# An encoder trunk on one core: the cross-attention's output product by seven block products, and the order of all engines written out

## The chip, the core and the metric

One Trainium2 chip, and of it one core. The core has five engines with an instruction queue each: TensorE (PE; its weight loads are shown as PEld), VectorE (DVE), ScalarE (ACT), GpSimd (POOL) and SyncE (SP), which here does nothing but issue transfers. The metric is the device time of one execution in microseconds (us).

## The reference, cut to what matters

Two layers over x (512 rows of 1024), each with a mixer, a cross-attention into 256 memory rows and an MLP, all in float32:

```python
for l in range(DEPTH):
    h = rms_norm(x, g_mix[l]); z = h @ w_in[l]
    ...                                   # differential attention and a two-way linear recurrence
    x = x + jnp.concatenate([o, r], axis=-1) @ w_out[l]

    hq = rms_norm(x, g_xq[l]); m = rms_norm(mem, g_mem[l])
    qx = (hq @ xa_wq[l]).reshape(B, S, X_HEADS, X_HEAD_DIM)   # 4 heads of 256
    ...
    p = jax.nn.softmax(s, axis=-1).astype(vx.dtype)
    ox = jnp.einsum('bhsm,bmhd->bshd', p, vx).reshape(B, S, D_MODEL)
    x = x + ox @ xa_wo[l]                 # the product that the change is about

    hm = rms_norm(x, g_mlp[l])
    x = x + jnp.square(jax.nn.relu(hm @ mlp_w1[l])) @ mlp_w2[l]
return rms_norm(x, g_final)
```

## The kernel before

**Layout and tiles.** x is kept transposed: eight chunks `c_x0` to `c_x7` of 128 features by 512 rows. A weight tile is 128x1024, one column block of 128 outputs for all eight chunks of the contraction. Each float32 operand is split into a high part and a low part in a format that TensorE multiplies at speed, and a product is three matmuls (high·high, high·low, low·high). A weight arrives by a transfer in a `wraw` buffer (3 of them); ACT writes its high part to `whi` and DVE the rest to `wlo` (3 of each). `b` is a pool of 62 tiles of 128x512, `pt` one of 4, `mm` and `at` are the 3 + 5 banks of PSUM, into which TensorE writes.

**The cross-attention's output product** (called the XO stage below). `residual_fm` forms chunk m of `ox @ xa_wo`: 8 chunks of the contraction by 3 matmuls of 512 columns into one bank, then one DVE addition into `c_x`. The eight operands `ox` come from `XHead.pv`, two a head: PSUM is split at once into a high and a low tile. After each chunk `prep_x` splits the new x for the MLP (one ACT, one DVE instruction) and adds its square for the norm (one of each).

**Seven block products** (`seven`, line 1093 on) are already there for the MLP's second product. A pair of chunks of the contraction and both halves of the 512 rows make a 2x2 block matrix, and so does a pair of weight tiles; seven products of blocks do what eight did. `left_pair` makes the sums and differences of the activations (`a`, `kh/kl`, `s`, `u`), `right_pair` those of two weight tiles (`whi`, `wlo`, and `pt` for the intermediate sums). A product is 4 pairs by 3 matmuls of 256 columns. The seven run in three banks X, Y and Z; product 6 goes on in bank X on top of product 1, so it follows the DVE addition that reads product 1 out.

**Order.** Every operation is recorded by `Plan.record`, in the order of the program. `Plan.schedule` then places them with its own table of costs, by a key for each (time of recording less a lead; `ahead(...)` sets leads for loads, splits and attention, and `LEADS` holds one more for each operation). `Plan.emit` writes out the order found; each engine takes its own instructions in that order, and each waits for what it reads and for its buffers. All of them carry line 490, so the rows below are told apart by tile names.

Of the kernel before, what the change touches and what calls it, by code (L numbers as in the profile page):

```python
# [18 lines left out]
P = 128  # L19
S = 512  # L20
# [29 lines left out]
ATT_AHEAD = 3  # L50
SPLIT_AHEAD = 18.0
LOAD_AHEAD = 105.0
CAST_AHEAD = 28.0
NEG_AHEAD = 20.0
# [3 lines left out]
LEAD_STEPS = '#$%&()*+,-./0123456789:;<=>?@ABCDEFGHIJKLMNOPQRSTUVWXYZ[]^_`abcdefghijklmnopqrstu'  # L58
LEADS = (
    'uL63BCuGGgGGGG@@<<HGuue>d>auFOMu9Q-ZAAGA-2D-H)?NNOC*@%AD?EA#6&/,0,?CBBB,=5>BBDFA?1J1C-G;JF$80?FUFKP;'  # L60
    'eOD?AK9NLPBWOOZ``Y[S^YcRURQTTRQNPLNNNTJJPIJJLISQR[XMMXXOGHOJFMMABIQPVUkUU[[[WTPSSLLJLuuLRSCNRJJJKJEG'
    'GVSXQNMECF>lK`LLJIJIKKNK```KCDDIDcCjL[YSeY_Ua0^NGLLGGLIGP>LEU@@D@0L4HHKKPutukM<=tYfYfBKOPKuuuu[uTZuK'
    'JOOHTtmqtmufuuFCVbmuDDM7MRLCZrruuu0&u?;;;K6CDC4uuuuuuCuuuuMussuguuuuKIDQa>OEYC;>X@<EgqlsultlllutluPQ'
    'QVV:Wqo^^ZQQF25BGIuuuuuuuuuuNZknIBNEKiWuuuuuuuuuutuusGGA:LJGN_quU_lYYYVuuuuuubuuuubuuuudsuuu_lonEbab'
    'QkdkGWhmmS^E_aetGFV`UmiusL7U1UaaUoOJJkVV`N_MJCEEGRFHHHRKFMDLJJKJ@@@MDMJCHDNHHGHHHRGPHKOOHGOHHHVHLAIP'
    'KKKTLTTHHHI6IL>CCRI:RI5JLJV@HPGH;JC;>IGKHDFFCFHFHCFBBBAB@@HIOED_RLLQLEREHEHISTWVTH`VLLJLLMILGLLLMP_^'
    'LLLWUL^LOHJPXLrRWRffVRLPJOOLAPPPNKP_QOFOLOIWFWYMPW]RLRRLLLLLLLLLVLULLULLULLLLLLLLLLVLQSUNLLLELCLILLH'
    'TOOPOO[OOGA@IA@A@KKIKGIKGMIGGILNKJLRPQLLLKKLJLLOLRLLMJLKLLLLLILKKLHHHCH8I8HI8HHHLLI8LLILLLLLLI8LSSSS'
    'SLL8I8L8ILJIJJJLCJLMJLLPLLHLOLLKNLLLLCLALK>LLLLLK<LH>LLLLLK>LLQNN@GQLGKLLNMLQQLPNKKLPJJLKHLVL[LL>RIJ'
    'LLMEOFFGFEW5VU2[VWF$ZZ#W#KG)JDHDFJQ#n]5U^Ru:ufaX`7b2X5pCbGdYQ_RRVAF[Ac[]qsqnoqrPgXHdS=g5LkBTOKGG_?Gu'  # L70
    '<GJIIAbMUASrUMqMb`L`MTMMMMNNNXeZ_ZndVOTTMZMZdeghZZXUMZZZZZZZUUUYUKZSZ[bbbbeeKeJiIK^J]]XUVNQQ=R=IFFJL'
    'LNKKKKWKLJOLLNMLMNLOONNLOLLNNLLONNLLLLOOMONONQLLQMLCLOOOLLSLLMONLONSNLLLLLHLMLFFFILMOLNLFFILNHGLLLLK'
    'LNLMMKLLNLNNLXMLXLLXMLLNLLLMLMXNLLYLLMXLNLMLIXXHLHLLLLHXXHHLIXDLLLLKLLLDUFLQDKQLFELLILCCCFCOEKBBDPEE'
    '>PDDDBR?>PPUBBGBP<<>B>C>H:HCCCICHH<JI>GD=DCDCJDC?>?????>@>AFFFFGQPFFFDBFFFF?>?FB?F@@9<@;@@@FLFFLFLHL'
    'HLLHLLHHJLLHLLLHHHGHLHLBHLLLMLLMLFLJKKKLLLLLLNLLLLLLLLLLLLKLLLLLLLLLLLLLLLLLLLLLLLLNLLLLLLMKLLLLLLLL'
    'MLLLLMLKLLKLLLLLLMLLLLMKLMLLLLLKLLLMLMLMSLLLKMLRTSUSRRRRRRRSRRQQRRRRRRRRRRWRWRRORTQMRVVRWRVTMRRMVSRR'
    'RRRRRRTRRRRRSRRTRRRTOTSSSRRTRXSMIR^RPSSLMLKRNLIQ_YPPU`oRJRVUW]WU^[VVMZZMZMMM]]W]XWVVPOVGuuuuujd^kjhZ'
    'mmmmmmtsphqhi`iemeSWjjkijm[udfSupuqiuuuqjutieabuunuuuuuuuuucrpcurrrruUUuuea0]]a-h9hrrrrurrrrbruuuuoo'
    'ouUuussuUWWTuuuuuuVLuuuu2nio,a7euuuugqu[r>^aaaFR=LGHLLLLHLSVLLLLLLMLLZnLLD@EE:E:9`ELTCKKKK9====11110'
    '10==:1/EEA9EEFE6EBNZEEEEEEE9-E48NNIHNINIE@EFEEDFDFE>E<EE>NNHQUUUUABBEEW_VLLKKLMKJKILLLMKJLJLLJLLLLLL'  # L80
    'LLLLELJHLOOLOQLMF<A@@FHHFT;T;IM8KLLLLOX_XFEO@FLNKJLMOLCAFF9KNDH@A@AWIIXuaiVtccTQZPiYVY_WuuuJPSNraRuq'
    'sUsPP`eIJDC?jqmmCDEYaAJCWJJJA?8uTS`LV^^a<fnIe=_TbQ=SSY[IZZWWCfuTECGPVm^WOiA=.===igukHbXVh>LLLLLLLILD'
    'TILJLLLILLRLTQLLLFLDGLLNLALNLONNMWMNMSYSXNJ`CC=>U=???V;:ECXKPPPLMCPPHDDIJBGJAKLKGHFJXKRNGMMMPSSTSSPK'
    'KQMMFOOMOMMMTHGJVHRMMMMSKMOUPGVOSGOPSPNKRE^UV^[[[[[^>UH`^]`UUUUUT><T2OUOPT=OBON;JQLLQXZXOMDTDTOSWZsq'
    'cje<FaN````SUIRI?ZrsEEPDNDHJjOmnguhunuucc[[qtcfk`uupmuum]]X^uuuuaVL]dhZe]]_ojrcuuuuuuuuuuaahuug`oktu'
    'uuutkhbbbusinVTYofODlQ@7lOTGodhkMUjajDTMGgh`JLHZ5QG9m/2:6OR888D;;dZCERCCCEGE@<@:B@:::B@G?>>G>;CCDCCH'
    'G>NPNN@RUTB5B;5?;<;7;;B8;B;8BBFGIAII@>>;><99>>>9>9H?>GGGGGGNMB7D7>ABRMHHOKA?G@GBGJCBNBMBJE=B[NcNcEEd'
    'O?aREEuuuuuuuuWJuu[eH;u;R36Lcm/JHPA?M2Y:IWYt`PPPuPPRQUPPSPVIccicPcce]Rubl[RPHVL@VEXXuuDSluJNKSSQuPPP'
    'NPPSTQ_bnf^WXWRWoJGERPAPBPWL]ZG?QITFGLPHRJcGY]hYWJdNbPUPZgUTf_XZZ_uY[[SZ[u`n_bZHRRJegaXFD[>[=^3_SS1V'
    'LIEiQH-S2$tnneC^ReSNGHH>H7><;THHEHMHHB>P=C@HOFTQDLHeHQdOVUUMMYWY_jQYeeXMMMM_eMMMMMKMKK_bMKKKKaaVVVLQ'  # L90
    'WcWLdLWLSLXNNPPPRQPPP[P_WP[RSP[PE[[[[____GCGPPP[WPWWPPPVVPPRPPD>BCPJWPPOPPPPPCURCO=SXPYSRQIIINIIXV^Q'
    '``SFSPEDAAEELRWTZdMIMNMSSTSOTUOd^WV[XLJLLOLLJ]]ORUUGQFO[MGGGGGGFF*#WaUYa[DSbJLhLoK<UMEKL4UCJa0X/U*%&'
    '[###M###M%%+FOurMuuuruA.mP(S888?=EKHUT_M*MMPLSiuQlaJouuB*=Auuuuuuuuquusu777VAu@qQXWFUXZ.-5=AAEEE???D'
# [1469 lines left out]
```

## Time and profile before

| | us |
|---|---|
| median of 3 runs (lowest, highest) | 1463.85 (1462.7, 1465.16) |
| the profiled execution, whole / its span | 1463.46 / 1461.7 |
| TensorE busy | 1430.8 (98% of the span) |
| VectorE busy | 1108.0 (76%) |
| ScalarE busy | 758.2 (52%) |
| GpSimd busy | 41.5 (3%) |

The span runs from the first instruction to the last of one execution. "Busy" counts an instruction from its start to its modelled end; since matmuls overlap in the pipeline, a busy TensorE need not be one at its fastest.

### The profile page before, as it was taken

The numbers are of one execution on the slowest core, as the hardware profiler recorded it, in microseconds if no ns is written. First come the engines' busy times: TensorE is split into PE (matmuls) and PEld (weight loads), VectorE is DVE, ScalarE is ACT, GpSimd is POOL, SyncE is SP. The second block draws the span as 40 slices with busy tenths as digits, with TensorE's granted clock in tenths as the row PEclk, the third lists the DMA queues.
The fourth block names the chain that finished last, engine by engine and source line by source line (L and its number), as shares of the span: only waits on it lengthen the run. The fifth ranks groups of instructions, "written<-read, shape, count | busy, mean of one in ns | idle before, by whom it ended". The sixth has DMA issues, their size and how long they took to land.

```text
span 1461.7 us, 20808 instructions
## 1 busy us (share of the span) xinstructions
PE 1430.8 (98%) x8054; PEld 1228.4 (84%) x8054; DVE 1108.0 (76%) x1891; ACT 758.2 (52%) x1164; POOL 41.5 (3%) x69
## 2 busy tenths in 40 slices
PE   8999999999999999999999999999999999999997
PEld 6777887888889889898987779888888898989986
DVE  7889886564679697797958999755655786959786
ACT  6598755443445353444536887644443544435352
POOL 1000000000000000000000011000000000000001
PEclk9999999999999999999999999999999999999998
DMA  6454643221323233233334565422122233232322
GB/s 204 116 144 106 183 159 90 98 72 38 108 87 102 101 102 101 101 102 101 101 115 113 145 167 166 132 87 87 59 71 87 101 102 115 74 115 90 119 81 72
DMA packets 50258, 157.67 MB, mean 108 GB/s; under 512 B 6384, under 2 KB 8560, under 8 KB 50160
## 3 DMA queue, kind: packets, MB, share of 16 engines
q1 hardware_dynamic: 47136, 145.61, 31.1%
q0 software_dynamic: 2880, 10.49, 3.4%
q8 instruction: 63, 1.03, 0.3%
q14 instruction: 35, 0.29, 0.1%
q10 hardware_dynamic: 144, 0.26, 0.0%
HBM read 141.65 MB, written 2.10 MB: 98 GB/s over the span
## 4 chain that ended last, share of the span: by engine, by line
PE 82%; DVE 10%; DMA 3%; ACT 3%; issue 1%; POOL 0%; SPq 0%; DVEq 0%; ACTq 0%; POOLq 0%
PE mm L490 63%; PE at L490 18%; DVE b L490 6%; DVE wlo L490 2%; ACT b L490 1%; DVE s L490 1%; DMA b<-b 1%; DMA wlo<-in_W 1%; ACT whi L490 1%; DVE pt L490 1%; DMA whi<-in_W 1%; DMA wraw<-in_W 0%; ACT L490 0%; POOL s L490 0%; SPq L490 0%
## 5 line engine op out<-in xcount | busy, mean ns | idle before, releaser
L490 PE MATMUL mm<-b,whi 128*128 128x512 f32 (+1 forms) x3640 | 976.4, 356 | 2.5 <-DVE b L490 1.7
L490 PEld LDWEIGHTS mm<-b,whi 128*128 128x128 f32 x3640 | 632.7, 188 | 107.6 <-ACT b L490 3.2
L490 PE MATMUL mm<-b,wlo 128*128 128x512 f32 (+1 forms) x1820 | 645.5, 355 | 1.7 <-DVE wlo L490 1.6
L490 ACT ACTIVATE whi<-wraw 128x1024 fp32r<-128x1024 f32 (+1 forms) x213 | 223.1, 1048 | 346.3 <-PE mm L490 186.8
L490 PEld LDWEIGHTS mm<-b,wlo 128*128 128x128 f32 x1820 | 342.3, 188 | 56.9 <-DVE wlo L490 2.8
L490 DVE TENSOR_TENSOR wlo<-wraw,whi 128x1024 fp32r<-128x1024 f32 (+1 forms) x213 | 257.1, 1208 | 41.3 <-ACT whi L490 40.3
L490 DVE TENSOR_TENSOR b<-b,b 128x512 fp32r<-128x512 f32 (+3 forms) x388 | 223.0, 594 | 10.1 <-ACT b L490 8.6
L490 ACT ACTIVATE b<-b 128x512 fp32r<-128x512 f32 (+2 forms) x288 | 168.8, 602 | 80.7 <-DVE b L490 78.0
L490 DVE SCALAR_TENSOR_TENSOR b<-mm,rb 128x512 f32<-128x512 f32 x80 | 55.2, 690 | 106.5 <-PE mm L490 105.7
L490 DVE TENSOR_TENSOR c_x<-c_x,mm 128x256 f32<-128x256 f32 (+1 forms) x160 | 74.5, 471 | 72.5 <-PE mm L490 71.9
L490 ACT ACTIVATE whi<-pt 128x1024 fp32r<-128x1024 f32 x64 | 67.6, 1060 | 98.9 <-PE mm L490 41.8
L490 PE MATMUL at<-b,whi 128*128 128x256 f32 x520 | 94.6, 278 | 0.0
L490 ACT ACTIVATE b<-at,s 128x512 f32<-128x512 f32 (+2 forms) x100 | 61.1, 615 | 45.6 <-DVE s L490 37.4
L490 PEld LDWEIGHTS at<-b,whi 128*128 128x128 f32 x520 | 79.6, 188 | 0.9
L490 DVE TENSOR_TENSOR wlo<-pt,whi 128x1024 fp32r<-128x1024 f32 x64 | 77.9, 1221 | 2.9 <-ACT whi L490 2.7
L490 PE MATMUL at<-b,wlo 128*128 128x256 f32 x260 | 72.4, 278 | 0.1
L490 PE MATMUL at<-b,b 128*128 128x256 f32 (+1 forms) x320 | 65.7, 331 | 4.7 <-DMA b<-b 3.9
L490 DVE TENSOR_REDUCE s<-at 128x1 f32<-128x512 f32 (+1 forms) x80 | 54.6, 687 | 16.8 <-PE at L490 16.6
L490 PEld LDWEIGHTS at<-b,b 128*128 128x128 f32 x320 | 47.4, 190 | 12.7 <-DMA b<-b 4.8
L490 PE MATMUL at<-b,pt 128*128 128x256 f32 x384 | 53.8, 278 | 0.0
L490 PE MATMUL at<-pt,b 128*128 128x256 f32 (+1 forms) x288 | 50.0, 319 | 2.2 <-DVE pt L490 2.2
L490 DVE TENSOR_TENSOR c_x<-c_x,at 128x256 f32<-128x256 f32 x97 | 39.5, 417 | 13.9 <-PE at L490 13.4
(127 smaller groups left out, 1234.8 us busy)
## 6 DMA issues: line engine op xcount, KB each, us to landing
wraw<-in_W SPq DMA_DIRECT2D x239, 512.0 KB, 3.3
b<-b SPq DMA_DIRECT2D x96, 128.0 KB, 2.5
whi<-in_W POOLq DMA_DIRECT2D x10, 512.0 KB, 4.0
wlo<-in_W POOLq DMA_DIRECT2D x10, 512.0 KB, 5.5
wraw<-in_memT SPq DMA_DIRECT2D x4, 512.0 KB, 5.4
out_T<-b SPq DMA_DIRECT2D x16, 128.0 KB, 1.8
c_x<-in_xT SPq DMA_DIRECT2D x7, 256.0 KB, 6.2
wraw<-in_W SPq DMA_DIRECT2D x6, 256.0 KB, 4.5
```

Of the source, the lines that this page charges most:

```text
L490: getattr(self.engines[op.eng], m)(*a, **k)
```

## The change

For each layer the XO stage is formed by `seven`, four times for a pair of chunks. `XHead.pv` no longer splits the two halves of a head's output: ACT copies the first out of PSUM, and `left_pair` makes the block operands. And the scheduler is gone: `order` takes each operation's place from a table, `ISSUE`, of which two characters name an operation. The table covers the whole program, not the XO stage alone. The numbers of buffers and the rest of the arithmetic stay.

```diff
-LEADS = (
-    'uL63BCuGGgGGGG@@<<HGuue>d>auFOMu9Q-ZAAGA-2D-H)?NNOC*@%AD?EA#6&/,0,?CBBB,=5>BBDFA?1J1C-G;JF$80?FUFKP;'
...
+ISSUE = (
+    '###,#<#*#+#8$b#:%q#)H*&>#%#&#(&?#.#-#7#0#$#1#/#4#5%)#=$c#K#>#C#2#6#9#;%*$q#D%-#L$9$:$;$<$d$e$f$g#E#O'
...
-    def schedule(self):
-        ops = self.ops
...
+    def order(self):
+
+        at = [DIGITS.index(a) * 90 + DIGITS.index(z) for a, z in zip(ISSUE[::2], ISSUE[1::2])]
+        assert sorted(at) == list(range(len(self.ops)))
+        place = {self.ops[i]: p for p, i in enumerate(at)}
+        for op in self.ops:
+            assert all(place[p] < place[op] for p in op.preds | op.behind if p is not op)
+        return sorted(self.ops, key=place.get)
...
-                hi, lo = R(), R()
-                split(hi, lo, pm)
-                out.append((hi, lo))
-            return out
+                out.append(pm)
+            te = T()
+            A.activation(te, out[0], AF.Copy)
+            return left_pair(te, out[1])
...
-            ox += hd.pv()
+            ox.append(hd.pv())
...
-        for m in range(8):
-            residual_fm(l, T_XO + m, ox, m)
-            xs[m] = prep_x(l, "g_mlp", m, nrm)
+        for m in range(0, 8, 2):
+            seven(l, T_XO + m, T_XO + m + 1, ox, m, m + 1)
+            for c in (m, m + 1):
+                xs[c] = prep_x(l, "g_mlp", c, nrm)
...
-    order = plan.schedule()
-    plan.emit(tc, order)
+    plan.emit(tc, plan.order())
```

**Place 1, the start of the XO stage in layer 0.** TensorE, before: the end of head 3's product with the memory values (`pt`), then chunk 1 (bank `mm_3491`) and chunk 2 of the output product.

```order
L490 MATMUL at_3518<-pt_3489,b_2517 128x512
L490 MATMUL at_3518<-pt_3495,b_2517 128x512
L490 MATMUL at_3518<-pt_3489,b_2524 128x512
L490 MATMUL mm_3491<-b_3409,whi_3347 128x512
L490 MATMUL mm_3491<-b_3418,whi_3347 128x512
L490 MATMUL mm_3491<-b_3409,wlo_3359 128x512
L490 MATMUL mm_3534<-b_3089,whi_3390 128x512
```

TensorE now: `at_3550` is head 3's second half, `at_3411` is bank Y (product 5), `mm_3399` bank X (product 1 with `whi_3334`, then product 6 with `whi_3237`), `at_3491` bank Z (product 2).

```order
L390 MATMUL at_3550<-pt_3495,b_2792 128x512
L390 MATMUL at_3411<-b_3522,whi_3237 128x256
L390 MATMUL at_3411<-b_3546,whi_3237 128x256
L390 MATMUL at_3411<-b_3522,wlo_3380 128x256
L390 MATMUL mm_3399<-b_3544,whi_3334 128x256 x2
L390 MATMUL mm_3399<-b_3544,wlo_3338 128x256
L390 MATMUL mm_3399<-b_3228,whi_3237 128x256
L390 MATMUL mm_3399<-b_3241,whi_3237 128x256
L390 MATMUL mm_3399<-b_3228,wlo_3380 128x256
L390 MATMUL at_3491<-b_3519,whi_3334 128x256
```

The end of product 1 (head 3's part, `b_3544`) now stands four groups behind head 3, and product 6 into the same bank right behind it.

VectorE at the same place, before: an addition into `c_x`, one weight's low part, one `prep_x` split, and so on, a chunk at a time.

```order
L490 TENSOR_TENSOR c_x_0_66<-c_x_0_66,mm_3420 128x512
L490 TENSOR_TENSOR wlo_3560<-wraw_3252,whi_3552 128x1024
L490 SCALAR_TENSOR_TENSOR b_3570<-c_x_0_66,c_prm_70,b_3558 128x512
L490 TENSOR_TENSOR c_x_1_74<-c_x_1_74,mm_3491 128x512
L490 TENSOR_TENSOR wlo_3591<-wraw_3370,whi_3583 128x1024
L490 SCALAR_TENSOR_TENSOR b_3602<-c_x_1_74,c_prm_70,b_3589 128x512
```

VectorE now: head 3's `left_pair` (`b`), the additions (`c_x`), the last weight of the first pair (`wlo_3583`), and the sums of the second pair's weights (`pt`).

```order
L390 TENSOR_TENSOR b_3562<-b_3562,b_3542 128x256
L390 TENSOR_TENSOR c_x_0_68<-c_x_0_68,mm_3399 128x256
L390 TENSOR_TENSOR b_3559<-at_3550,b_3562 128x256
L390 TENSOR_TENSOR b_3581<-b_3562,b_3565 128x512
L390 TENSOR_TENSOR wlo_3583<-pt_3234,whi_3557 128x1024
L390 TENSOR_TENSOR c_x_1_98<-c_x_1_98,mm_3399 128x256
L390 TENSOR_TENSOR b_3600<-b_3559,b_3598 128x512
L390 TENSOR_TENSOR c_x_1_98<-c_x_1_98,at_3411 128x256
L390 TENSOR_TENSOR wlo_3633<-wraw_3625,whi_3631 128x1024
L390 TENSOR_TENSOR pt_3651<-wraw_3625,wraw_3623 128x512
L390 TENSOR_TENSOR b_3653<-at_3550,b_3629 128x512
```

The first pair's other weights, and three quarters of the heads' operands, stand further ahead, between the attention's own instructions.

**Place 2, the end of the XO stage in layer 0.** TensorE, before: chunk 7 ends (`mm_3756`), then the MLP's first product begins (`mm_3795`).

```order
L490 MATMUL mm_3756<-b_3522,whi_3682 128x512
L490 MATMUL mm_3756<-b_3527,whi_3682 128x512
L490 MATMUL mm_3756<-b_3522,wlo_3690 128x512
L490 MATMUL mm_3795<-b_3558,whi_3721 128x512
L490 MATMUL mm_3795<-b_3570,whi_3721 128x512
```

TensorE now: `at_3946` is the last pair's product 3, `mm_3990` the MLP's first product, `mm_3879` the last pair's product 7.

```order
L390 MATMUL at_3946<-b_3250,pt_3937 128x256
L390 MATMUL mm_3990<-b_3858,whi_3971 128x512
L390 MATMUL mm_3990<-b_3941,whi_3971 128x512
L390 MATMUL mm_3990<-b_3858,wlo_3973 128x512
L390 MATMUL mm_3990<-b_3856,whi_3971 128x512
L390 MATMUL mm_3990<-b_3860,whi_3971 128x512
L390 MATMUL mm_3990<-b_3856,wlo_3973 128x512
L390 MATMUL at_3946<-b_3382,pt_3937 128x256
L390 MATMUL at_3946<-b_3443,pt_3937 128x256
```

The MLP's first product now begins between the last pair's products.

**Place 3, the first attention head of layer 0.** SP before: copies of the key parts (`b` from `b`), with a weight load between the last two.

```order
L490 DMA b_599<-b_569 64x512 x2
L490 DMA b_605<-b_574 64x512
L490 DMA wraw_611<-in_W 128x1024
L490 DMA b_605<-b_574 64x512
L490 DMA wraw_668<-in_W 128x1024
```

SP now, the same copies (other numbers):

```order
L390 DMA b_588<-b_546 64x512
L390 DMA b_592<-b_546 64x512 x2
L390 DMA b_584<-b_550 64x512
L390 DMA wraw_627<-in_W 128x1024
L390 DMA wraw_629<-in_W 128x1024
```

The weight load has moved behind the last copy.

## Rows read from the trace of the kernel before

**Rows 1.** Page, part 1: engine, busy us (share of span), instructions.

```profile
PE 1430.8 (98%) x8054; PEld 1228.4 (84%) x8054; DVE 1108.0 (76%) x1891; ACT 758.2 (52%) x1164; POOL 41.5 (3%) x69
```

**Rows 2.** Windows: stretch, its length, each engine's busy us (instructions), clock, DMA.

```profile
5.00:60.00 55.00, 52.61 (x225) 41.93 (x226) 44.41 (x119) 31.19 (x50) 2.93 (x5) 1.00 0.62 187
60.00:230.00 170.00, 162.64 (x875) 135.56 (x875) 151.76 (x273) 129.78 (x222) 11.17 (x19) 0.99 0.51 139
344.00:395.00 51.00, 51.00 (x234) 41.66 (x233) 28.38 (x42) 20.71 (x35) 0.00 (x0) 1.00 0.24 83
446.40:502.50 56.10, 56.10 (x413) 52.71 (x412) 43.01 (x71) 21.87 (x27) 0.00 (x0) 1.00 0.26 85
800.00:915.00 115.00, 110.40 (x627) 93.84 (x626) 109.72 (x189) 96.25 (x155) 9.89 (x9) 1.00 0.56 156
1062.00:1111.00 49.00, 49.00 (x216) 39.57 (x215) 27.43 (x40) 20.29 (x34) 0.00 (x0) 1.00 0.23 75
1406.80:1449.10 42.30, 41.47 (x350) 40.23 (x348) 36.23 (x65) 19.08 (x26) 0.70 (x1) 1.00 0.12 38
```

**Rows 3.** Windows with matmuls of 512 columns (first) and 256 columns (others).

```profile
949.84:997.51 47.67, 47.67 (x207) 38.44 (x205) 28.70 (x36) 20.30 (x28) 0.00 (x0) 1.00 0.29 93
1254.04:1288.03 33.99, 33.99 (x301) 33.99 (x300) 29.61 (x51) 14.30 (x16) 0.00 (x0) 1.00 0.30 94
538.06:570.25 32.19, 32.19 (x277) 32.19 (x276) 29.36 (x50) 14.15 (x16) 0.00 (x0) 1.00 0.29 99
```

**Rows 4.** Timeline of DVE, last MLP block: start, us, engine, line, operation, count.

```profile
1414.76 0.41 DVE L490 TENSOR_TENSOR c_x<-c_x,mm 128x256 f32<-128x256 f32 x1
1415.09 0.68 DVE L490 TENSOR_TENSOR pt<-pt,wraw 128x512 f32<-128x512 f32 x1
1415.69 0.41 DVE L490 TENSOR_TENSOR c_x<-c_x,at 128x256 f32<-128x256 f32 x1
...
1416.36 1.22 DVE L490 TENSOR_TENSOR wlo<-pt,whi 128x1024 fp32r<-128x1024 f32 x1
1417.49 0.41 DVE L490 TENSOR_TENSOR c_x<-c_x,mm 128x256 f32<-128x256 f32 x1
```

**Rows 5.** Timeline of DVE in the XO stage, layer 0.

```profile
367.54 0.74 DVE L490 SCALAR_TENSOR_TENSOR b<-c_x,c_prm,b 128x512 fp32r<-128x512 f32 x1
368.20 1.22 DVE L490 TENSOR_TENSOR wlo<-wraw,whi 128x1024 fp32r<-128x1024 f32 x1
```

**Rows 6.** Groups by form: count | busy us, mean ns | idle before, releaser.

```profile
L490 PE MATMUL mm<-b,whi 128*128 128x256 f32 x1272 | 229.2, 280 | 0.3 <-DVE c_x L490 0.2
L490 PEld LDWEIGHTS mm<-b,whi 128*128 128x128 f32 x3640 | 632.7, 188 | 107.6 <-ACT b L490 3.2 <-issue 1.7 <-DVE b L490 1.0
L490 ACT ACTIVATE whi<-wraw 128x1024 fp32r<-128x1024 f32 x207 | 219.4, 1061 | 346.1 <-PE mm L490 186.8 <-issue 124.4 <-PE at L490 27.0
L490 ACT ACTIVATE b<-at 128x512 fp32r<-128x512 f32 x16 | 9.6, 598 | 14.8 <-PE at L490 14.7
L490 ACT ACTIVATE b<-b 128x256 fp32r<-128x256 f32 x32 | 13.3, 417 | 0.9
L490 ACT ACT_TABLE_LOAD x30 | 38.5, 1283 | 1.7 <-PEq L1558 1.2
```

**Rows 7.** Waits of PE: engine <- whom, us in total, times, longest.

```profile
PE at L490 <- DVE s L490: 5.6, 3, 4.2
PE at L490 <- DMA b<-b: 3.9, 4, 1.7
```

**Rows 8.** Timeline of SP and PE at the first head's scores.

```profile
53.96 0.53 SPq L490 DMA_DIRECT2D wraw<-in_W  x1
54.53 0.46 SPq L490 DMA_DIRECT2D b<-b  x1
...
58.82 0.47 PE L490 MATMUL at<-b,b 128*128 128x512 f32 x1 [1.34 <-DMA b<-b]
```

More of the change, by code (lines that the diff above doesn't have):

```diff
@@ L1 @@
-import bisect
-import heapq
 import math
@@ L203, in __init__ @@
         self.tag, self.shape, self.dtype, self.name = tag, list(shape), dtype, name
-        self.log, self.left, self.tile, self.slot, self.end = [], 0, None, None, 0.0
+        self.log, self.tile = [], None
 class _Op:
-    __slots__ = ("eng", "calls", "dur", "key", "idx", "npred", "succ", "ready", "roots", "new",
-                 "table", "start", "end", "bytes", "preds", "behind")
+    __slots__ = ("eng", "calls", "dur", "idx", "roots", "preds", "behind")
 class _Engine:
@@ L302, in record @@
             op.eng, op.calls, op.dur, op.idx = eng, [], 0.0, len(self.ops)
-            op.succ, op.roots, op.new, op.ready, op.preds, op.behind = {}, [], [], 0.0, set(), set()
-            op.table, op.bytes = None, 0
-            op.key = self.t - self.lead
+            op.roots, op.preds, op.behind = [], set(), set()
             self.ops.append(op)
@@ L314, in record @@
             self.t += c
-        if m == "dma_start":
-            v = out[0] if out else k["in_"]
-            op.bytes = 4
-            for d in v.shape:
-                op.bytes *= d
-            if "accum_op" in k:
-                op.bytes *= 2
-        if m == "activation":
-            op.table = self.SETS.get(str(a[2]).split(".")[-1])
         for v in allv:
@@ L330, in record @@
                 op.roots.append(r)
-                r.left += 1
                 if not r.log:
-                    op.new.append(r)
                     r.first = op
@@ L542, in raw_weight @@
                 cs = slice(h * 512, h * 512 + 512)
[L543 to L547 removed]
+                SP.dma_start(out=raw[:, cs], in_=W[l * NT + t][:, cs])
+        else:
+            SP.dma_start(out=raw, in_=W[l * NT + t])
         return raw
@@ L554, in weight_dma @@
         src = W[l * NT + t]
-        with plan.ahead(CAST_AHEAD):
-            G.dma_start(out=hi, in_=src)
-        with plan.ahead(NEG_AHEAD):
-            A.activation(lo, b(hi), AF.Copy, scale=-1.0)
-            G.dma_start(out=lo, in_=src, accum_op=ALU.add)
+        G.dma_start(out=hi, in_=src)
+        A.activation(lo, b(hi), AF.Copy, scale=-1.0)
+        G.dma_start(out=lo, in_=src, accum_op=ALU.add)
         return hi, lo
@@ L570, in weight @@
         lo = plan.tile("wlo", [P, 1024], F32R)
-        with plan.ahead(SPLIT_AHEAD):
-            for cs in (slice(0, 512), slice(512, 1024)) if first else (slice(0, 1024),):
-                split(hi[:, cs], lo[:, cs], raw[:, cs])
+        for cs in (slice(0, 512), slice(512, 1024)) if first else (slice(0, 1024),):
+            split(hi[:, cs], lo[:, cs], raw[:, cs])
         return hi, lo
@@ L601, in trunk @@
     prm = C([P, NPAR], F32, "prm")
-    with plan.ahead(1000.0):
-        SP.dma_start(out=prm, in_=par)
+    SP.dma_start(out=prm, in_=par)
     post = C([P, 4], I32, "post")
@@ L607, in load_x @@
     def load_x(c, q):
-        with plan.ahead(900.0 - c):
-            q.dma_start(out=x[c], in_=xT[c * P:(c + 1) * P, :])
+        q.dma_start(out=x[c], in_=xT[c * P:(c + 1) * P, :])
     def pc(l, name, i):
@@ L1144, in mem_load @@
             m = plan.tile("wraw", [P, 1024], F32)
-            with plan.ahead(LOAD_AHEAD):
-                SP.dma_start(out=m, in_=memT[:, 1024 * i:1024 * (i + 1)])
+            SP.dma_start(out=m, in_=memT[:, 1024 * i:1024 * (i + 1)])
             out.append(m)
@@ L1398, in trunk @@
                 hd = Head(h, heads[h], vt, nlam, gsub)
-            with plan.ahead(ATT_AHEAD):
-                hd.scores(qc)
+            hd.scores(qc)
             fill(FILL[l][u] / 2)
-            with plan.ahead(ATT_AHEAD):
-                step()
+            step()
             later(LAG, lambda hd=hd, qc=qc: hd.turn(qc))
@@ L1410, in trunk @@
         while todo:
-            with plan.ahead(ATT_AHEAD):
-                step()
+            step()
         while fill(100.0):
```

374 lines of the change are left out of this document (143 added, 231 removed).

## The prediction

> **What bounds the kernel now.** I read the shares first. TensorE is busy for 1430.8 of 1461.7 us [rows 1], so the sum of its instructions is the time, and a gain must come from fewer or shorter matmuls or from its 30.9 us of idle time. VectorE at 76% and ScalarE at 52% bound nothing as averages. The stretches then tell where that is not so [rows 2]. In the two XO stages (344 to 395 and 1062 to 1111 us) TensorE is never idle, and VectorE is busy for little more than half of the time: pure matmul time. In the attention of layer 0 (60 to 230) TensorE is idle for 7.4 us while VectorE is busy for 151.8 of 170; in that of layer 1 (800 to 915) the figures are 4.6 idle and 109.7 of 115. There VectorE is nearly the bound, and only the order decides what TensorE waits for. In the MLP the seven products are already in use: 446.4 to 502.5 has no idle time on TensorE, 1406.8 to 1449.1, the last block, 0.8 us. Those two stretches are the nearest thing to the XO stage after the change.
>
> **What the change removes from TensorE.** A pace is read where matmuls of one size stand alone, by the count of weight loads, one a matmul [rows 3]: 47.67 us for 205 of 512 columns is 0.2325 us each; 33.99 us for 300 of 256 columns is 0.1133, and 32.19 for 276 is 0.1166. I take 0.115 for the small ones. The XO stage of a layer was 8 chunks x 8 x 3 = 192 matmuls of 512, or 44.6 us. It becomes 4 pairs x 7 products x 4 x 3 = 336 of 256, or 38.6 us (38.1 to 39.2). That is 6.0 us less a layer (5.4 to 6.5), 12.0 for both (10.8 to 13.0).
>
> The number of weight loads rises by 144 a layer, each of 188 ns [rows 6]. They cost nothing where 300 of them run beside 300 matmuls in 33.99 us [rows 3]. The Trainium skill speaks against this: its page "TensorE: Matmul & The Clock Gate", section "Back-to-back issue gap", says that in a stream of load and matmul both set the spacing, and gives some 81 ns for 128 columns and 131 for 512. An estimate on the line between them is 98 ns for 256, and by it a layer would go from 25.2 to 32.8 us, 15.4 us more for both. This trace disagrees with both the level and the ratio: 0.2325 against 0.115 is 2.0 to 1.
>
> **What it adds on VectorE.** Steps are read from start to start where instructions follow at once [rows 4, 5]: 128x1024 takes 1.13 us, 128x512 0.60, 128x256 0.33, and the `prep_x` split 0.66. A pair of weight tiles cost 2 x 1.13 = 2.3 us; it costs 3 x 1.13 + 5 x 0.60 = 6.4. The additions into `c_x` go from 2 x 0.60 to 7 x 0.33 = 2.3 a pair. A head's operands go from 2 x 0.60 to 5 x 0.33 + 3 x 0.60 = 3.45. For 8 pairs and 8 heads that is 33 + 9 + 18 = 60 us more, 1108 to 1168, some 80% of the span. All of this lies beside TensorE, if it is spread well.
>
> In the XO stage itself it is not obvious. A pair with its two `prep_x` (2 x 1.26) needs 6.4 + 2.3 + 2.5 = 11.2 us on VectorE against 84 x 0.115 = 9.7 on TensorE. So for four pairs VectorE has 44.9 us to do. From the row of the first addition on (place 1), 5.3 us of the first pair's weights are already done ahead, 2.1 us of head 3's operands and 2.3 us of the MLP's first two weights are to be added: 44.0 us. TensorE has by then some 8 groups of three (2.8 us) behind it, so 35.8 us of XO are left, and then 14 of 16 groups of the MLP's first two products, which need only the first seven chunks: 14 x 3 x 0.2325 = 9.8 us. That is 45.6 us of cover for 44.0 us of work. The order does use it: at place 2 the MLP's first product stands between the last pair's products. So the stage is nearly in balance, with no wait by the sum, but with little slack: a late weight here and there shows on TensorE. One wait is written into the order: at place 1 product 6 follows product 1 in the same bank, so it waits for a matmul's 0.28 us [rows 6] and an addition's 0.41 [rows 4], less the step of 0.115, some 0.6 us. Bounds for the idle time that this adds in a layer: nothing, as in 446.4 to 502.5 (336 small matmuls at 0.115 and 77 large at 0.2325 are 56.5 us for 56.1), and 3.7 us, if all of 42.3 less 38.6 in the last MLP block [rows 2] was idle or spent on waits (its 14 short matmuls take a part of it). I take 2.0 a layer, between the two because the XO stage has more VectorE work than the one and more cover than the other: 4.0 for both.
>
> **The hand-over from head 3.** ACT now copies the first half out of PSUM (0.60) and then writes `a` (0.42) before the last group of product 1 can start [rows 6]: 1.0 us, while TensorE still has six matmuls of 512 and three of 256 (1.7 us). Hidden; uncovered it would cost 1.0 us a layer. ScalarE in all: one 1024 (1.06) and half of one more a pair, 1.7 us more a head, some 25 us over the program, and two more table loads of 1.28 [rows 6] (32 against 30 in the order). At 52% they hide; in the attention of layer 0, where ACT is busy for 129.8 of 170, the table loads could cost up to 2.6 us. The transfers are the same in number and size.
>
> **What the new order does elsewhere.** It moves nearly everything, and no row tells its worth as a whole. Below: it can remove at most the idle time of the attention, 7.4 + 4.6 us, and 2.4 more in 5 to 60 [rows 2]. Above: the same order of size as a loss. What can be read in it: TensorE's longest wait for a copy (3.9 us in 4 waits [rows 7]) includes 1.34 us for one issued at 54.53, behind a weight load issued at 53.96 that took 0.53 us of the queue [rows 8]. At place 3 that weight load now stands behind the copies. The 5.6 us for small VectorE results [rows 7] lie for 4.2 us at the very start and stay. I take 3.0 us off, a quarter of the 12.0, since one wait is visibly treated and the others I can't price.
>
> **Sum.** 1463.46 (the profiled execution's own time, 0.4 below the median, 1.8 above its span) - 12.0 + 4.0 - 3.0 = 1452.5; I say 1452.
>
> **Rivals.**
> - *The order gains more than the products.* It spreads VectorE's work better in both attentions, and two thirds or more of the 14.4 us of idle time from 5 to 60, 60 to 230 and 800 to 915 go. For it: VectorE is not fully busy even there, and place 3. Against it: 151.8 of 170 leaves little. Time: 1463.5 - 12.0 + 4.0 - 9.6 = 1446, down to 1440 if the XO stages also run without idle time.
> - *VectorE becomes the bound of the XO stage, and the products' gain is gone.* Were the MLP's start no cover (its weights or chunks late), 44.0 us of VectorE stand against 35.8 of TensorE: 8.2 us a layer given back, 16.4 in all. Time: 1463.5 - 12.0 + 16.4 - 3.0 = 1465, no change. For it: 11.2 against 9.7 us a pair, and only three `whi`, so no second pair can be prepared ahead. Against it: place 2.
> - *Slower: VectorE's queue holds TensorE up in the attentions.* Each engine takes its instructions strictly as the table has them; where one of VectorE's waits for a matmul that now stands later, what TensorE needs queues behind it. Place: 60 to 230 and 800 to 915, with some 5 us of VectorE slack in the second. It decides from the point where their idle time grows from 12.0 by the 8.0 us that XO leaves plus 2.9 us, to 23. If it more than doubles, to 27: 1463.5 - 8.0 + 15.0 = 1470. For it: nothing but the tightness of these stretches. Against it: the few rows that I can price moved the right way.
> - *Weight loads set the pace of small matmuls.* 336 x 0.188 = 63.2 us a layer against 44.6: 37 us more, 1500. The page of the Trainium skill named above would have the change lose too, by less. The 300 in 33.99 us exclude it nearly.
>
> **Chances.** The forecast 0.60, with a range of its own from 1447 to 1459 (XO idle time from 0 to 3.7 a layer, the pace by 1, the order from -6 to 0); more from the order 0.18; the XO gain gone 0.10; slower by the attentions 0.11; weight loads 0.01. 0.2% is 2.9 us, about what the measurement can tell from no change: faster is below 1460.9, slower above 1466.8. Faster: 0.60 + 0.18 = 0.78; same 0.10; slower 0.12. For 8 in 10 the range goes from 1440, where the second case ends, to 1465, the case with the gain gone; the slower cases and the ends of these two are left out.
>
> **What would show it.** Right: 336 matmuls of 256 columns more a layer for 192 of 512 fewer, at 0.113 to 0.117 us; TensorE idle by 1 to 4 us in each XO stage, at the hand-over and by late weights (`wlo`, `c_x` as releasers); VectorE near 1168 us; the XO stage some 41 us of TensorE's time instead of 44.6; and the 1.34 us at the first scores gone or halved. Wrong: TensorE waiting for `wlo` or `pt` in every pair of the XO stage (the second rival); idle time beyond 23 us in the two attentions (the third); a pace above 0.12 us in the XO stage (the fourth).

## The result, and the profile after

The changed kernel takes 1442.87 us (median of 4 runs, 1441.76 to 1444.51) against 1463.28 for the kernel before on the same chip: a ratio of 0.9861 [0.9844, 0.9879], 1.4% faster. Forecast were 1452, and a range from 1440 to 1465. The profiled execution took 1441.76 us, 1440.0 of it span; that of the kernel before 1463.46 and 1461.7. So 21.7 us are to be explained, and 11.0 of them were forecast.

The page of the changed kernel, part 1, beside [rows 1]:

```profile
PE 1417.3 (98%) x8342; PEld 1244.8 (86%) x8342; DVE 1160.8 (81%) x2027; ACT 778.0 (54%) x1206; POOL 44.3 (3%) x69
```

There are 288 matmuls more, as the change says, and VectorE has 1160.8 us to do (1168 forecast). TensorE's busy time fell by 13.5 us, its idle time on the page from 30.9 to 22.7.

TensorE's waits in the changed kernel, in the columns of [rows 7]:

```profile
PE at L390 <- DVE s L390: 6.3, 3, 4.1
PE mm L390 <- ACT whi L390: 1.8, 1, 1.8
...
PE mm L390 <- DVE c_x L390: 0.8, 2, 0.6
```

No wait for a copy is listed any more; in [rows 7] it was 3.9 us. The wait for `c_x` is the one written into the order at place 1. It can be seen there, on TensorE, at the start of the XO stage of layer 0:

```profile
341.62 0.41 PE L390 MATMUL mm<-b,whi 128*128 128x256 f32 x2
341.87 0.28 PE L390 MATMUL mm<-b,wlo 128*128 128x256 f32 x1
342.77 0.51 PE L390 MATMUL mm<-b,whi 128*128 128x256 f32 x2 [0.62 <-DVE c_x L390]
```

One wait has two sizes here. From start to start there are 0.90 us where a step of this size is 0.12: 0.78 us are lost. The bracket says 0.62, since it counts from the modelled end of the matmul, 0.28 us after its start, and the next one could have started long before that end.

This matters for every window. Below are stretches with the same work before and after, by their first and last matmul (columns as in [rows 2]). Before: the attentions of layers 0 and 1.

```profile
5.96:223.58 217.62, 210.45 (x1077) 173.67 (x1077) 191.46 (x382) 156.35 (x262) 14.10 (x24) 0.99 0.52 148
728.04:944.44 216.40, 211.45 (x1134) 177.59 (x1133) 184.35 (x323) 153.72 (x246) 15.20 (x19) 1.00 0.49 138
```

After: the same two, and behind them the two XO stages, each with the MLP's first products that follow it (72 matmuls of 512 columns in layer 0, 33 in layer 1).

```profile
6.46:214.02 207.56, 204.75 (x1070) 173.03 (x1071) 189.54 (x380) 160.62 (x264) 16.08 (x25) 1.00 0.52 154
713.97:926.67 212.70, 210.45 (x1135) 178.87 (x1133) 186.86 (x325) 153.21 (x247) 14.55 (x19) 1.00 0.51 146
...
328.20:391.71 63.51, 62.47 (x458) 58.69 (x457) 59.67 (x108) 35.73 (x57) 0.30 (x1) 1.00 0.19 67
1043.21:1093.21 50.00, 49.68 (x378) 47.17 (x377) 48.68 (x89) 28.42 (x42) 0.00 (x0) 1.00 0.32 106
```

Layer 0's attention is 10.1 us shorter with the same matmuls (but for six small ones, some 0.5 us), though by busy time it had only 7.2 us of idle time to lose. So I count idle time from the starts instead: for every matmul, the time to the next start, less the step of its size (0.2322 us at 512 columns, 0.1178 at 256; for the 438 smaller matmuls some 0.11 at 128 columns and 0.06 below, and other values for these move both kernels alike), where more than 0.03 is left. By that count the attention of layer 0 had 19.1 us of idle time and has 9.6: 12 gaps above 0.25 us with 9.5 us in all became 6 with 4.4, and 105 smaller ones with 9.6 us became 70 with 5.2. Stages and the whole program, in us of idle time by this count:

| stage | before | after |
|---|---|---|
| attention, layer 0 / layer 1 | 19.1 / 11.4 | 9.6 / 7.6 |
| output product of the mixer, layer 0 / 1 | 2.6 / 0.5 | 0.7 / 0.5 |
| XO stage, layer 0 / 1 | 0.6 / 0.7 | 2.8 / 2.0 |
| last MLP block | 6.9 | 4.8 |
| all | 48.4 | 33.7 |

14.7 us of the gain are idle time by this count; the other 7.0 are matmul time. The count takes in matmuls at the lower of TensorE's two clocks, too: 1.7 of the 19.1 us are no wait, but a stretch of 3.41 us at half clock near 168 us (shown in the last section). And the idle time went from the attentions, which the new products don't touch, while it grew by 3.5 us in the XO stages, which they do.

The steps of matmuls changed too, everywhere. Two stretches of the changed kernel with 512 and with 256 columns, beside [rows 3]:

```profile
936.26:980.00 43.74, 43.74 (x192) 35.56 (x190) 26.91 (x36) 19.46 (x27) 0.00 (x0) 1.00 0.28 96
1230.89:1264.46 33.57, 33.57 (x287) 33.57 (x285) 29.65 (x49) 15.70 (x19) 0.00 (x0) 1.00 0.29 97
```

By the starts, 188 steps in the first are 0.2310 us each and 285 in the second 0.1178. Over the program the means are 0.2311 and 0.1179, against 0.2329 and 0.1150 before.

### The profile page after: what moved, and what is told of

It reads as the page before. It is cut to its first block, busy times and chain, and to the rows that moved or that the text cites. A ratio compares the mean times of both kernels' runs of the same rounds, so it can differ in the third digit from the quotient of the medians.

```text
span 1440.0 us, 21582 instructions
## 1 busy us (share of the span) xinstructions
PE 1417.3 (98%) x8342; PEld 1244.8 (86%) x8342; DVE 1160.8 (81%) x2027; ACT 778.0 (54%) x1206; POOL 44.3 (3%) x69
## 4 chain that ended last, share of the span: by engine, by line
PE 89%; DVE 9%; issue 1%; ACT 1%; DMA 1%; POOL 0%; DVEq 0%; ACTq 0%
PE mm L390 66%; PE at L390 23%; DVE b L390 6%; DVE wlo L390 1%; DVE s L390 1%; DVE pt L390 0%; DMA wraw<-in_W 0%; ACT b L390 0%; DMA c_prm<-in_par 0%; ACT L390 0%; ACT whi L390 0%; DVE c_x L390 0%; ACT pt L390 0%; POOL s L390 0%; ACT rb L390 0%
## 5 line engine op out<-in xcount | busy, mean ns | idle before, releaser
L390 PE MATMUL mm<-b,whi 128*128 128x512 f32 (+1 forms) x3640 | 943.2, 347 | 1.9 <-ACT b L390 1.0
L390 DVE TENSOR_TENSOR b<-b,b 128x512 fp32r<-128x512 f32 (+3 forms) x420 | 240.6, 590 | 18.0 <-ACT b L390 15.1
L390 PE MATMUL at<-b,whi 128*128 128x256 f32 x648 | 122.9, 282 | 0.0
L390 DVE TENSOR_TENSOR wlo<-pt,whi 128x1024 fp32r<-128x1024 f32 x80 | 97.6, 1222 | 12.1 <-ACT whi L390 11.2
L390 PEld LDWEIGHTS at<-b,whi 128*128 128x128 f32 x648 | 100.3, 188 | 1.6
L390 PE MATMUL at<-b,wlo 128*128 128x256 f32 x324 | 91.5, 283 | 0.6 <-DVE wlo L390 0.6
L390 PE MATMUL at<-b,pt 128*128 128x256 f32 x480 | 74.7, 281 | 0.0
L390 PEld LDWEIGHTS at<-b,pt 128*128 128x128 f32 x480 | 66.0, 189 | 2.1 <-DVE c_x L390 0.2
L390 PEld LDWEIGHTS at<-b,wlo 128*128 128x128 f32 x324 | 62.1, 192 | 1.0 <-DVE wlo L390 1.0
L390 DVE TENSOR_TENSOR pt<-pt,wraw 128x512 f32<-128x512 f32 x80 | 54.9, 687 | 0.7
```

The lines of the kernel that those rows point to most:

```text
L390: getattr(self.engines[op.eng], m)(*a, **k)
```

## The experiments

Theory A: the new order gained most, in the attentions (13 us and more), and the products 6 to 8. Theory B: the sizes of the prediction (order 3.0), so the products would have gained the rest.

**First tries: order alone and products alone.** In the first, the old product's instructions were put at the places of the new ones in the new table:

```diff
-            ox.append(hd.pv())
+            ox += hd.pv()
...
-        for m in range(0, 8, 2):
-            seven(l, T_XO + m, T_XO + m + 1, ox, m, m + 1)
...
+        for m in range(8):
+            residual_fm(l, T_XO + m, ox, m)
```

> The output product stays as it was before (eight chunks, 512 columns); all other operations stand in the new order, and the eight chunks are put where the seven products' instructions stood. Theory A (the order removes idle time in the attentions, about 13 us, and the products add some 7 us on top): 1450 us, from 1447 to 1453, and TensorE's idle time in the attention of layer 0 half of before. Theory B (my prediction's sizes: the order 3 us, the products the rest): 1460 us, from 1458 to 1463.

In the second, the table of the kernel before took in the new products:

```diff
-    '###,#<#*#+#8$b#:%q#)H*&>#%#&#(&?#.#-#7#0#$#1#/#4#5%)#=$c#K#>#C#2#6#9#;%*$q#D%-#L$9$:$;$<$d$e$f$g#E#O'
+    '#,#)###*#-#($u#+#.#%&*#0#/#>#1#&%)$q#<%-H9%*H=#6%q$b#2#8#=#7&+$c#9#3#4%r#?#5#:#$$d#A$e#CH*$f#;#B#K$g'
...
```

> The seven products are in; everything outside the cross-attention and the first four tiles of the MLP stands in the order of before, the cross-attention itself in the new one. Theory A: 1463.3 less 8 (12 less of matmul time, 3.4 to 4 more idle time in the two XO stages) gives 1455 us, from 1452 to 1458. Theory B: the seven products carry nearly the whole of the gain, 1443 to 1449 us.

Measured: 1479.23 (ratio 1.0093 [1.0079, 1.0107]) and 1654.13 (1.1286 [1.1269, 1.1303]). Both missed every expectation, by my placing. TensorE's largest wait of each, the first kernel's and then the second's:

```profile
PE mm L385 <- DVE c_x L385: 17.8, 6, 4.8
```

```profile
PE at L390 <- DVE b L390: 59.5, 24, 7.6
```

In the first, the additions of the old chunks stand where those of the pairs had stood, too late; 32.7 us of idle time lie in the two XO stages. But its attentions are idle for 10.9 and 8.0 us, as after. In the second, the rule by which I gave instructions the changed kernel's places also caught scores of the self-attention; 87 and 66 us of idle time lie in the two attentions. It tells nothing of the products.

**Each kernel again.** No edit, on the same chip, to see what varies from one execution to the next.

> The changed kernel as it is, on the same chip as the two above. Both theories: 1443 us, from 1441.5 to 1444.5. If the pace of matmuls (0.2311 us for 512 columns, 0.1178 for 256 in its first trace) belongs to the program, the trace shows it again within 0.0005; if it belongs to the single execution, it differs by 0.002 or more, as it did between the traces of before and after.

> The kernel before, once more, for its trace. If the pace belongs to the program: 0.2333 and 0.1149 us again. If to the execution: another pair. The stretch of 3.4 us at half clock near 168 us comes back if the idle time ahead of it (1.3 us at 160 and 0.7 at 164) decides it, and need not if it is chance.

Measured: the changed kernel 1442.72 (ratio 0.9843 [0.9829, 0.9856]), 34.6 us idle in its profile; the kernel before, one run, 1467.92, 49.4 us idle, 19.5 and 12.3 of it in the attentions. The idle times repeat within 1.7 us a stage. The steps of the changed kernel repeat to 0.0001 us; those of the kernel before at 512 columns too, but its 256 columns took 0.1161 on the mean instead of 0.1150.

**Order alone, with the old product in its own order.** From the start of the query product (first kernel) or of the output product (second) up to the MLP's first products, the instructions keep the order of the kernel before among themselves; everything else keeps the new one. The code is that of the first try; the table differs.

> The new order everywhere, with the old output product (8 chunks of 192 matmuls of 512 columns a layer) put back in the order that the kernel before has inside the cross-attention and up to the MLP's first products; the tiles keep the places in memory that the changed kernel gives them. Theory A (the order was worth far more than the 3 us forecast, most of it idle time in the two attentions; the products about 7): 1447 to 1451, and TensorE idle for 9 to 11 us and 7 to 8 us in the attentions of layers 0 and 1, as in the changed kernel, against 19 and 11 before. Theory B (the sizes of the prediction, order 3): 1459 to 1461, idle times near those of before.

> As the run with the new order and the old output product, but TensorE keeps the new order through the query product too, and only the output product itself, up to the MLP's first products, stands in the order of the kernel before. So the loss at the start of layer 0's query product (9.1 us idle there) should go. Theory A (order 13 to 18 us, products net some 6 to 8): 1447 to 1451. Theory B (order 3): 1459 to 1461. Had the earlier run's time been the order's own worth and not the seam's: 1456 to 1459.

Measured: 1458.96 (0.9957 [0.9943, 0.9971]) and 1461.21 (0.9978 [0.9969, 0.9987]). As totals they fit Theory B, or nothing. By stage they don't. The first one's attentions, and its query product in layer 0, with the joint:

```profile
6.51:214.18 207.67, 204.84 (x1071) 173.15 (x1072) 189.82 (x380) 160.66 (x264) 16.06 (x25) 1.00 0.54 154
263.58:340.56 76.98, 71.34 (x358) 59.17 (x356) 45.68 (x74) 30.61 (x61) 1.01 (x1) 0.98 0.19 62
...
725.47:937.67 212.20, 210.45 (x1134) 178.87 (x1133) 186.97 (x325) 153.14 (x247) 14.59 (x19) 1.00 0.53 147
```

The attentions take 207.67 and 212.20 us, as in the changed kernel, with the old product: their gain is the order's alone. Idle time by starts is 9.6 and 7.1 there. At the joint between the two orders 9.1 us are idle where the changed kernel has 0.7. Less these 8.4 us, the profiled execution (1455.94, the fastest of the five) would stand at 1447.5 and the median at 1450.6; the second kernel, with 13.2 us more than usual in its joints, at 1448.0. All lie in Theory A's range, but by subtraction.

**Products alone, the rest in the order of before.** The counterpart: the changed kernel's code, the order of before outside the stretch.

> The seven block products in the cross-attention, with their order from the changed kernel between the query product and the MLP's first products, and the order of the kernel before everywhere else. Theory A: the products alone are worth about 7 us (12 by the old pace of 0.115 for 256 columns, less 3 to 4 of idle time, and some mismatch at the seams): 1454 to 1458, attentions idle as before (19 and 11 us). Theory B (the order did only 3, the products the other 17): 1446 to 1448.

Measured: 1472.14 (1.0045 [1.0032, 1.0058]), slower than the kernel before and outside both ranges. Layer 0's attention, and TensorE's largest wait:

```profile
5.90:224.47 218.57, 210.95 (x1076) 173.99 (x1077) 191.47 (x382) 156.49 (x262) 14.09 (x24) 0.99 0.52 147
```

```profile
PE mm L390 <- ACT whi L390: 8.1, 2, 6.9
```

Its attentions are idle for 19.9 and 10.7 us, as before. The XO stages run as after, with 3.3 and 2.3 us idle. The joints are bad again: 7.0 us by the starts lie in that one wait of layer 1's MLP, where a weight's high part comes late, and 14.9 us in all more than before. Less these, 1457.2: the products alone are worth some 8 us. Again by subtraction.

**The old order in one attention only.** The stretch takes in the mixer's output product behind layer 0's attention. It has its joint where little is in flight, so the total can be read directly. The tiles are kept where the changed kernel has them.

```diff
       with tc.manual_schedule():
+        for tag in ("b", "wraw", "whi", "xb", "s", "wlo", "at", "mm"):
+            r = next(r for o in order for r in o.roots if r.tag == tag)
+            self.pools[tag].tile(r.shape, r.dtype, tag=tag, bufs=self.count[tag], name="first_" + tag)
         for op in order:
...
-    '###,#<#*#+#8$b#:%q#)H*&>#%#&#(&?#.#-#7#0#$#1#/#4#5%)#=$c#K#>#C#2#6#9#;%*$q#D%-#L$9$:$;$<$d$e$f$g#E#O'
+    '#,#)###*#-#($u#+#.#%&*#0#/#>#1#&%)$q#<%-H9%*H=#6%q$b#2#8#=#7&+$c#9#3#4%r#?#5#:#$$d#A$e#CH*$f#;#B#K$g'
```

> The changed kernel with the order of the kernel before for the attention of layer 0 up to the query product of the cross-attention, and the new order from there on; the tiles keep the places of the changed kernel. Theory A: TensorE's idle time in this stretch goes back from 9.6 to about 19 us, and the time to 1450 to 1455. Theory B (the order matters little there): 1443 to 1446.

Measured: 1452.97 (0.9921 [0.9907, 0.9935]), 10 us above the changed kernel, in the middle of Theory A's range. The stretch in its windows, layer 0's attention and then layer 1's:

```profile
5.92:222.03 216.11, 209.09 (x1074) 172.74 (x1075) 191.58 (x381) 156.53 (x261) 14.16 (x23) 1.00 0.52 149
723.44:935.51 212.07, 210.39 (x1134) 178.93 (x1133) 187.01 (x325) 153.14 (x247) 14.56 (x19) 1.00 0.53 147
```

216.11 us against 207.56, with 17.7 us of idle time, and the mixer's output product behind it, also in the old order, takes 50.8 us against 49.4; layer 1 stays at 212. So the order of this one stretch is worth some 10 us, three times what I gave it in the whole program. The amount of VectorE's work there is nearly the same (191.58 and 189.54), so it is the order that counts; of which engine, this run doesn't tell, since it put back the old order of all.

**Where the tiles lie.** In all runs above but the last, the step that a matmul takes went with the order: 0.2311 and 0.1179 us wherever the new table begins the program, 0.2329 and 0.115 to 0.116 wherever the old one does. In the last one the old order begins, but the tiles lie as in the changed kernel, and the steps are 0.2311 and 0.1178. The pools place their tiles at first use, so the table also decides where they lie. In the kernel before, by the addresses of the program, `b` begins at 672 modulo 2048 bytes and `whi`, `wlo` and `pt` at 1504; in the changed kernel `whi` at 672 too. The edit is the one above, with `wraw, b, xb, s, at, whi, wlo, mm` in the first kernel and `b, wraw, whi, wlo, pt, xb, s, at, mm` in the second, which brings all of them to 672. The banks of PSUM are the same in all four.

> The changed kernel, order and products as they are; only the places of the tile pools in SBUF and PSUM are fixed in the order in which the kernel before first uses them (wraw, b, xb, s, whi, wlo instead of b, wraw, whi, xb, s, wlo). Theory P (the steps of a matmul depend on where its tiles lie): 512 columns go from 0.2311 to 0.233 us a step, 256 columns from 0.1178 to 0.1136 to 0.116, so 3776 x 0.0018 = 6.8 us more and 4128 x 0.002 to 0.003 = 8 to 12 less: 1437 to 1442. Rival (the steps depend on the instructions' order, not on places): 0.2311 and 0.1178 stay, 1442 to 1444.

> The changed kernel with the tile pools placed in the order b, wraw, whi, wlo, pt, then xb and s, so that wlo and pt lie at the same offset in 2048 bytes as whi and b. Theory P2 (the step of a matmul of 512 columns is 229 ns where the weights loaded lie at the offset of b, 233 to 234 where not; in the changed kernel whi does and wlo doesn't): the third step falls to 229 too, 3776 x 0.0018 = 6.8 us less if the 256 columns stay at 0.1178, so 1435 to 1438. Rival (another of the places sets the step, or 256 columns get slower by as much): 1441 to 1445.

Measured: 1442.90 (0.9849 [0.9835, 0.9863]) and 1439.65 (0.9828 [0.9814, 0.9841]). Stretches of 512 and then 256 columns in the first, which has two kinds of the latter:

```profile
934.94:978.81 43.87, 43.87 (x190) 35.16 (x189) 26.65 (x36) 19.42 (x27) 0.00 (x0) 1.00 0.30 96
440.79:471.74 30.95, 30.95 (x275) 30.94 (x273) 27.62 (x48) 13.39 (x16) 0.00 (x0) 1.00 0.32 103
1230.73:1264.30 33.57, 33.57 (x287) 33.57 (x286) 29.55 (x48) 15.71 (x19) 0.00 (x0) 1.00 0.28 97
```

And in the second:

```profile
934.43:977.07 42.64, 42.64 (x190) 35.29 (x188) 26.45 (x35) 19.43 (x27) 0.00 (x0) 1.00 0.30 99
1227.81:1262.00 34.19, 34.19 (x287) 34.19 (x285) 29.88 (x49) 15.69 (x19) 0.00 (x0) 1.00 0.28 95
```

With the old places the old steps return in the new order: 188 steps of 0.2333 us, 273 of 0.1134 and 285 of 0.1178 (means 0.2330 and 0.1159). With all of them at one offset the steps are 0.2268 and 0.1200 (means 0.2278 and 0.1198). So the places set the steps, and the two sizes go opposite ways. Neither pair of expectations held as a whole: the first total lies in the range of its rival, though the steps went as Theory P has them, since 256 columns won less than its sum asks for; the second lies between Theory P2 and its rival, which was half right. At the old places 3776 matmuls of 512 lose 7 us and 4128 of 256 win 8, and the time stays. At one offset 12.5 us are won and 7.8 lost. The second kernel's runs (1438.14 to 1439.93) lie below all of the changed kernel's, the lowest of which is 1441.76. This version is faster than the changed kernel by some 3 us.

**Place 2: the MLP's products out from between the output products.** TensorE's rows in layer 0, a part. The rows taken out here stand behind the last output product instead: four groups of three matmuls in layer 0 (2.8 us) and two groups in layer 1 (1.4 us), not four in each as the expectation has it.

```diff
 L390 MATMUL at_3946<-b_3250,pt_3937 128x256
-L390 MATMUL mm_3990<-b_3858,whi_3971 128x512
-L390 MATMUL mm_3990<-b_3941,whi_3971 128x512
-L390 MATMUL mm_3990<-b_3858,wlo_3973 128x512
...
 L390 MATMUL at_3946<-b_3382,pt_3937 128x256
```

> The changed kernel with one edit in the order of TensorE: in both layers the MLP's first four products stand behind the last product of the cross-attention's output instead of between its products. Prediction's step (VectorE has 44 us of work in the stage, which 35.8 us of output products alone don't cover): up to 8.2 us a layer more, so 1451 to 1459, with TensorE waiting for c_x, pt or wlo at the end of the stage. Rival (VectorE has done enough ahead, the MLP's products only fill): within 2 us of the changed kernel, 1441 to 1445.

Measured: 1444.98 (0.9866 [0.9852, 0.9879]), some 2 us above the changed kernel, not 8 to 16. The XO stages have 1.6 and 0.9 us more of idle time, and in the first of them the waits are these (in the changed kernel 0.8 us for `c_x` and 0.3 for `pt`):

```profile
PE mm L390 <- DVE c_x L390: 1.4, 3, 0.6
PE mm L390 <- ACT b L390: 0.5, 1, 0.5
PE at L390 <- DVE pt L390: 0.3, 1, 0.3
```

The added waits are single ones of 0.5 to 0.65 us, where the MLP's products had stood: these cover some 2 us, and as to the total the rival's range holds. But the run doesn't take away the cover that the prediction counted. It had put the MLP's first products behind the last output product, and there most of them stand in the changed kernel and all of them after the edit. In the changed kernel, from the first addition into `c_x` to the end of the last `prep_x` split of layer 0, and from the last output product to the end of the MLP's first products:

```profile
342.30:388.95 46.65, 46.02 (x349) 44.09 (x350) 44.33 (x76) 25.26 (x34) 0.00 (x0) 1.00 0.26 91
382.49:390.11 7.62, 7.62 (x35) 6.20 (x34) 7.25 (x12) 4.50 (x8) 0.00 (x0) 1.00 0.00 0
```

VectorE is busy for 44.33 of 46.65 us, and the last 6.5 us of that lie behind the output products, while TensorE has no wait in the MLP's. What would be lost without the MLP's products there, no run shows.

**Place 3: the load back ahead of the last copy.** The edit on SP:

```diff
+ L390 DMA wraw_595<-in_W 128x1024
  L390 DMA b_584<-b_550 64x512
- L390 DMA wraw_627<-in_W 128x1024
```

> The changed kernel with two of SyncE's transfers exchanged: the weight load at the first head's scores stands ahead of the last copy again, as in the kernel before. Prediction's step (the copy queued behind the load made TensorE wait 1.34 us): 0.5 to 1.4 us of idle time ahead of the first scores, 1443 to 1444.5. Rival (in the new order that copy is not the last thing the scores wait for): no idle time there, 1442 to 1443.5.

Measured: 1443.48 (0.9856 [0.9841, 0.9871]), which lies in both ranges; the rows decide. SP and then TensorE in this kernel:

```profile
52.53 0.53 SPq L390 DMA_DIRECT2D wraw<-in_W  x1
53.11 0.46 SPq L390 DMA_DIRECT2D b<-b  x1
...
54.03 0.40 PE L390 MATMUL mm<-b,wlo 128*128 128x512 f32 x1
54.26 1.53 PE L390 MATMUL at<-b,b 128*128 128x512 f32 x6
```

The copy stands behind the load again, as in [rows 8], and TensorE goes into the scores with no wait. The rival holds: the wait of 1.34 us went with the rest of the order, not with this exchange.

## Why the prediction was right, and by which step it was off

The direction and the range held, the size of the gain only by half: 1442.87 lies outside the forecast's own 1447 to 1459 and inside the wide range only because that took in the first rival. By the terms of the sum:

- **Matmuls of the XO stage, -12.0.** At the steps of before, 384 matmuls of 0.2329 us less and 672 of 0.1150 more are 12.1 us. Right. The 256 columns beside a weight load each run at 0.1178, so weight loads don't set the pace (0.188 would have shown). By the rule of the Trainium skill that the prediction weighed ("TensorE: Matmul & The Clock Gate", section "Back-to-back issue gap") these matmuls would, by the prediction's estimate, have cost 15.4 us more than before; steps of 0.231 and 0.118 us disagree with its figures after the change too.
- **The steps themselves, not in the sum.** I took the pace as a property of the size. At the changed kernel's tile places 4128 matmuls take 0.0029 us more and 3776 take 0.0018 less than in the profile before: 5 us back. Against the second execution of the kernel before it is 0.6, so that this term closes the sum is in part chance of the execution profiled.
- **Idle time in the XO stages, +4.0.** Measured 3.5. Right, and place 1 gives 0.6 of it by the page (0.8 by the starts), as said. The balance behind it held as well: for "45.6 us of cover for 44.0 us of work" layer 0 shows 46.65 us with VectorE busy for 44.33, the end of it under the MLP's products. Overrated was place 2 as the sign of that cover: of the 14 groups counted, only four stand between the output products in layer 0 and two in layer 1, worth some 2 us in all; the others follow behind. VectorE was nearly full in the stages (59.67 of 63.51, 48.68 of 50.00), and TensorE hardly waited.
- **The new order elsewhere, -3.0.** This is the step that failed, in its size: "I take 3.0 us off, a quarter of the 12.0". Idle time outside the XO stages fell by 18.2 us: 9.5 and 3.8 in the attentions, 2.1 in the last block, 1.9 in layer 0's output product of the mixer, 0.9 in sum in the rest. Of the 9.5, 1.7 are the stretch at the lower clock and not waits. The run with one attention and the output product behind it in the old order shows 10 us for that stretch alone. Even my upper bound, 14.4 us of idle time read from busy windows [rows 2], lay too low: by the starts the same stretches held some 30, since each modelled end covers the first 0.17 us or so of a wait.

In sum: -12.1 - 18.2 + 3.5 + 5 = -21.8, for 21.7 measured. That was the first rival's case, "the order gains more than the products", to which I gave 0.18, and whose own time of 1446 was still too high because it shared the bound.

The second rival (VectorE takes the XO gain) had the engine right, but its condition, that the MLP's start is no cover, didn't arise. What was called hidden was: in neither XO stage does TensorE wait for ScalarE's copy or its `a`, and with 778.0 us in all and two table loads more ScalarE gained 19.8, where 25 were forecast. The third (attentions slower) went the other way: their idle time fell from 30.5 to 17.2 us.

What stays open: which engine's rows in layer 0's attention bring the 10 us. What went was spread over many gaps (12 gaps above 0.25 us and 105 smaller ones became 6 and 70, some 15 of the small ones before at the lower clock), and no run took one engine's order alone. The exchange at place 3 is excluded. Nor is the order's worth as one total shown apart from the products: all five attempts at that lost 8 us or more in joints or by my placing; only the run on a single attention had no such loss.

## What to carry to other kernels

Where TensorE bounds a kernel, read its idle time from start to start of its matmuls, less the step of their size; the busy time of windows hides a part of every wait, here over half of those in layer 0's attention; stretches at the lower clock count as idle time in this way and are to be set apart. A change that rewrites the order of the whole program is to be priced with all of that idle time as its bound, whatever else the change says it does. And a table of order may decide where tiles lie: before putting a small difference down to the order, fix the places.

## What was not expected of the hardware

The step of a matmul depends on where its tiles lie in SBUF. With 512 columns it was 0.2329, 0.2311 and 0.2278 us, and with 256 columns 0.115 to 0.116, 0.1179 and 0.1198, for none, the high parts, and all of the weights at the offset of `b`, modulo 2048 bytes. That the places do it is shown; that this offset is what counts is not. Against it as the whole rule: where both operands are `b` tiles, which share the offset in every kernel, 512 columns took 0.2321 us in the kernel before and 0.2286 in the kernel with all tiles at 672. Within one triple of the changed kernel, the step from the matmul with `wlo` to the next with `whi` is 234 ns and the two others are 229; in the kernel before all three are 233. With the old places the 256 columns have two values, 0.1134 and 0.1178, which hold for whole stretches and differ from one execution to the next; why stays open.

The granted clock fell to the lower of its two levels (1.2 and 2.4 GHz) for 3.41 us once in each profile of the kernel before, ahead of the end, at 167.76 us in one and at 831.32 in the other. In the second, TensorE had waited for 2 us up to 830.98; the same wait in the first brought no fall, and there the last waits were one of 1.7 us up to 161.7 and one of 0.6 up to 165.2. Those came again in the second execution without a fall, and in the products-alone kernel with one at 167.90. What decides it stays open. The first:

```profile
167.76:171.17 3.41, 3.41 (x18) 3.41 (x17) 3.41 (x11) 1.08 (x3) 1.83 (x2) 0.50 0.83 288
```

In the last of the order-alone kernels, with waits of 2.9 us up to 302.7 and 2.8 up to 342.3, it fell for 6.83 us as the first ended and for 3.42 us some 1.1 us behind the second:

```profile
302.51:309.34 6.83, 6.59 (x18) 5.00 (x19) 1.82 (x2) 0.15 (x1) 0.00 (x0) 0.50 0.24 77
343.46:346.88 3.42, 3.42 (x15) 3.13 (x14) 1.43 (x3) 1.31 (x4) 0.00 (x0) 0.50 0.06 25
```

A stretch at the lower level costs about half of its length, 1.7 us for the first one shown and 3.3 for the 6.83 us here, on top of the wait. No profile of the changed kernel, or of its variants without joints, shows such a stretch ahead of the end.
